# Output projection to second FFN layer on one core: split weights get one place, the last layer begins where the operands lay, in three passes instead of two

## The chip, the core and the metric

The kernel runs on one core of a Trainium2 chip. The core has five engines that work side by side, each through its own list of instructions in order: TensorE (PE in the profile; PEld is its weight load), VectorE (DVE), ScalarE (ACT), GpSimd (POOL) and SyncE (SP, which here only starts transfers). Transfers between the chip's memory (DRAM) and the on-chip memory (SBUF) run on 16 DMA engines. Matrix products land in PSUM, eight banks of 2 KB per partition. The metric is the device time of one execution in microseconds (us); lower is better.

## The reference, cut to what matters

One trunk layer over 128 prompt and 1024 sample tokens (1152 rows of 1024), then a final norm. Four mixing branches are gated and merged; the stretch that the change touches starts behind that:

```python
x = x + g1 * (merged @ w_o)
h = rmsnorm(x, norm2_g) * (1 + s2) + b2
a, b = split(h @ ffn_w1)                       # 2 x 2816 columns
x = x + g2 * ((silu(a) * b) @ ffn_w2)
y = rmsnorm(x, final_norm_g)
```

All of it is in float32. The kernel gets float32 accuracy out of a faster matmul type (fp32r) by splitting every operand into a high and a low part: a product is three matmuls, high x high, high x low and low x high. A split is a cast on ACT (the high part) and a subtraction on DVE (the low part).

## The kernel before, in words

A scheduler orders the instructions: the program text gives each a place, and pools of SBUF tiles with a fixed number of buffers decide who must wait for whom. A tile of a pool is handed on when its last reader is done. `M(...)` takes one of eight 4.6 KB tiles per partition that live from the gates to the first FFN layer; a queue's transfers start in the order in which they stand.

- **Gates** (line 1137 on). For each branch and each of eight column blocks j: gate product, branch product, tanh, sum into `merged[j]`. In the last branch each finished block is halved and split into `mhl[j]`, the stationary operand of the next stage.
- **Output projection, "wo"** (from line 1436). Three chunks c of 384 rows, two column halves hf, four pieces k2 of `w_o`. A piece is loaded (512 KB, line 1243), split (ACT 1244, DVE 1245) and used by 18 matmuls. Behind each half, DVE multiplies by g1 (1457), POOL adds to x (1458), ACT sums squares (1459). Behind each chunk x is stored to DRAM (`x_d`, line 1461, on SP), then normalised in place (1470 to 1473).
- **Transposes into quarters** (`norm_to_quarters`, line 1264 on): PE transposes ("ntr"), ACT writes `nv` (1279), DVE and POOL form differences `nu` (1283 to 1286), and seven operands are split into `xa` and `xb` (1289, 1290).
- **FFN1** (from line 1291): 22 pairs of column blocks, each as seven block products (a Strassen-like scheme that needs sums S1 to S4 of the weights, made on POOL, line 1318). `w_prepare` loads, sums and splits the weights of a product some products ahead (`LEAD`). Pair 0 is done for chunks 0 and 1 first, then for chunk 2; pairs 1 to 21 follow whole. `evac` empties the banks into `st`, `store` splits the result and writes it to DRAM (`hid_d`, line 1405).
- **FFN2** (from line 1494): two passes over 11 of the 22 row blocks of `w_ffn2` each; in a pass nine row tiles i, each 11 x 3 x 2 = 66 matmuls into two banks; DVE multiplies by g2 (1551), POOL (first pass) or DVE (second) adds to `acc`, which is x read back from DRAM. The last pass ends with the norm and the output.

Between wo and FFN1, and between FFN1 and FFN2, pools are closed and opened in the same SBUF: a new pool's tiles wait for what lay there. Lines of before that matter:

```python
w = load_o(A["w_o"][hf, k2], M("wraw", [P, 1024]) if c == hf == 0 and k2 < 2 else slot("wraw"))
dma(x1_d[3 * c + q], x1s[q])                       # on SP
dma(hid_d[q, :, :, self.j, :]..., f(hl[q])...)     # on SP
fctx.__exit__(None, None, None)                    # behind the last product of FFN1
xctx.__exit__(None, None, None)
zctx = tc.tile_pool(name="zp", bufs=1, reuse_waits="tile")   # FFN2's pool
```

Of the kernel before, what the change touches and what calls it, by code (L numbers as in the profile page):

```python
# [15 lines left out]
P = 128  # L16
# [20 lines left out]
LEAD = 4  # L37
PASSES = ((0, 11), (11, 22))
# [46 lines left out]
def kernel(ctx: ExitStack, tc: tile.TileContext, A: dict, O: dict):  # L85
# [13 lines left out]
    mctx = tc.tile_pool(name="mp", bufs=1)  # L99
# [1022 lines left out]
    merged, mhl = [], []  # L1122
# [12 lines left out]
    def gates(name, step):  # L1135
# [5 lines left out]
        for j in range(8):  # L1141
            w = load_w(A["w_gate"][b, j], 1280)
            if step == 1:
                merged.append(M("mg"))
                dma(merged[j], m_d[j])
# [16 lines left out]
            if step == 3:  # L1162
                hl = []
                for q in range(2):
# [3 lines left out]
                    else:  # L1168
                        hl.append(M("mhl", dt=F32R).rearrange("p (c n) -> p c n", c=NCH))
# [64 lines left out]
    rowctx = tc.tile_pool(name="rows", bufs=1, reuse_waits="tile")  # L1234
    rows = rowctx.__enter__()

    def slot(name, dt=F32, shape=(P, 1024)):
        return rows.tile(list(shape), dt, tag="w", name=nm(name), bufs=8)

    def load_o(src, raw):  # L1240
        hi, lo = slot("whi", F32R), slot("wlo", F32R)
        with ahead():
            dma(raw, src)
            S.copy(hi, raw)
            V.tensor_sub(lo, raw, f(hi))
        return hi, lo
# [4 lines left out]
    xa = (xp.tile([P, 4, NCH, 4, HALF], F32R, tag="hT_hi", name="xa_hi", bufs=1),  # L1251
          xp.tile([P, 4, NCH, 4, HALF], F32R, tag="hT_lo", name="xa_lo", bufs=1))
    xbv = [t.rearrange("p o c (k n) -> p o c k n", k=4) for t in xb]
    OPS = {"B11": (xa, 0), "B21": (xa, 1), "T1": (xa, 2), "T2": (xa, 3), "T3": (xbv, 0), "T4": (xbv, 1), "B22": (xbv, 2)}
# [11 lines left out]
    def norm_to_quarters(xn3, c):  # L1266

        cs = c * CH
        for kp in range(4):
            v = M("nv", [P, 2, 2, HALF])  # L1270
# [22 lines left out]
    def ring(name):  # L1293

        if "fp" in wide:
            return wide["fp"].tile([P, 2, 512], F32R, tag="wf", name=nm(name), bufs=11)
        return slot(name, F32R, (P, 2, 512))
# [25 lines left out]
    def w_prepare(j, i):  # L1323
# [10 lines left out]
        t = ring("wf")  # L1334
# [386 lines left out]
```

## Time and profile before

| | us |
|---|---|
| median of 3 runs (range) | 2164.93 (2162.74 to 2166.24) |
| the profiled execution, its span | 2166.64, 2164.9 |
| end of the gates' last matmul | 1208.5 |
| last wo matmul | 1340.4 |
| first matmul of pair 1 | 1385.5 |
| end of FFN1's last matmul | 1857.6 |
| first FFN2 matmul | 1874.9 |
| last FFN2 matmul | 2156.5 |

Times within a run are us from the span's start. In the trace names are shortened: f is a bank of FFN1 or FFN2, x the rows x1, w a split block of w_ffn2, mg a block of merged. A view of waits says which engine waited for whom and how long; a table of windows gives for chosen stretches the busy time of each engine, the granted TensorE clock (PEclk, 1.00 is 2.4 GHz and 0.50 is 1.2 GHz) and what the DMA engines moved.

### The profile page before, as it was taken

The numbers are of one execution on the slowest core, as the hardware profiler recorded it, in microseconds if no ns is written. First come the engines' busy times: TensorE is split into PE (matmuls) and PEld (weight loads), VectorE is DVE, ScalarE is ACT, GpSimd is POOL, SyncE is SP. The second block draws the span as 40 slices with busy tenths as digits, with TensorE's granted clock in tenths as the row PEclk, the third lists the DMA queues.
The fourth block names the chain that finished last, engine by engine and source line by source line (L and its number), as shares of the span: only waits on it lengthen the run. The fifth ranks groups of instructions, "written<-read, shape, count | busy, mean of one in ns | idle before, by whom it ended". The sixth has DMA issues, their size and how long they took to land. (4 is left out here: it accounts for less than half of the span.)

```text
span 2164.9 us, 31502 instructions
## 1 busy us (share of the span) xinstructions
PE 2065.0 (95%) x12400; PEld 1845.0 (85%) x12400; DVE 1191.1 (55%) x2105; ACT 738.6 (34%) x1320; POOL 374.5 (17%) x308
## 2 busy tenths in 40 slices
PE   6899999999999999999999799799999999699998
PEld 1558888998897899999999677799999999578886
DVE  4833499825443288998732368665665655230323
ACT  3734444445432523322222245433333333110200
POOL 1210020000001102232212135332232221011100
PEclk9999999999999999999999899899999999899999
DMA  7684552234142452332210344233233322652431
GB/s 282 206 276 147 194 185 96 67 103 142 59 153 85 131 180 83 99 127 69 99 49 25 127 157 164 85 109 104 93 105 93 113 95 62 258 212 106 174 121 66
DMA packets 172233, 276.21 MB, mean 128 GB/s; under 512 B 14546, under 2 KB 123699, under 8 KB 171956
## 3 DMA queue, kind: packets, MB, share of 16 engines
q1 hardware_dynamic: 172084, 274.19, 37.7%
q8 instruction: 97, 1.59, 0.3%
q14 instruction: 52, 0.43, 0.1%
HBM read 196.58 MB, written 77.56 MB: 127 GB/s over the span
## 5 line engine op out<-in xcount | busy, mean ns | idle before, releaser
L257 PE MATMUL gm<-hT_hi,whi 128*128 128x384 f32 x1224 | 420.1, 343 | 1.7 <-ACT sg L1155 1.7
L259 PE MATMUL gm<-hT_hi,wlo 128*128 128x384 f32 x1224 | 418.6, 342 | 0.7 <-DVE wlo L233 0.7
L258 PE MATMUL gm<-hT_lo,whi 128*128 128x384 f32 x1224 | 415.8, 340 | 0.0
L257 PEld LDWEIGHTS gm<-hT_hi,whi 128*128 128x128 f32 x1224 | 230.0, 188 | 12.5 <-issue 7.5
L259 PEld LDWEIGHTS gm<-hT_hi,wlo 128*128 128x128 f32 x1224 | 230.0, 188 | 9.2 <-issue 5.1
L258 PEld LDWEIGHTS gm<-hT_lo,whi 128*128 128x128 f32 x1224 | 230.0, 188 | 5.7 <-issue 3.8
L1367 PE MATMUL f<-xa_hi,wf 128*128 128x288 f32 (+2 forms) x704 | 209.6, 300 | 9.1 <-ACT wf L1336 9.1
L1368 PE MATMUL f<-xa_lo,wf 128*128 128x288 f32 (+2 forms) x704 | 211.1, 301 | 2.0 <-DVE xa_lo L1290 1.9
L1369 PE MATMUL f<-xa_hi,wf 128*128 128x288 f32 (+2 forms) x704 | 207.4, 299 | 0.2 <-DVE wf L1337 0.2
L257 PE MATMUL f<-w,hid 128*128 128x512 f32 x396 | 152.2, 396 | 22.2 <-DMA hid<-hid_d 17.3
L1160 POOL TENSOR_TENSOR mg<-mg,sg 128x384 f32<-128x384 f32 x72 | 96.5, 1340 | 363.8 <-DVE sg L1156 359.4
L1367 PE MATMUL f<-xb,wf 128*128 128x288 f32 (+2 forms) x528 | 157.3, 298 | 0.0
L1369 PE MATMUL f<-xb,wf 128*128 128x288 f32 (+2 forms) x528 | 157.1, 298 | 0.0
L1368 PE MATMUL f<-xb,wf 128*128 128x288 f32 (+2 forms) x528 | 157.1, 297 | 0.0
L259 PE MATMUL f<-w,hid 128*128 128x512 f32 x396 | 154.5, 393 | 1.0 <-DMA hid<-hid_d 1.0
L258 PE MATMUL f<-w,hid 128*128 128x512 f32 x396 | 155.2, 393 | 0.0
L1367 PEld LDWEIGHTS f<-xa_hi,wf 128*128 128x128 f32 x704 | 134.2, 191 | 9.4 <-ACT wf L1336 9.2
L1155 ACT ACTIVATE sg<-gm,vec 128x384 f32<-128x384 f32 x96 | 55.8, 581 | 241.1 <-PE gm L259 231.9
L1368 PEld LDWEIGHTS f<-xa_lo,wf 128*128 128x128 f32 x704 | 134.7, 191 | 2.7 <-DVE xa_lo L1290 2.7
L1369 PEld LDWEIGHTS f<-xa_hi,wf 128*128 128x128 f32 x704 | 133.8, 192 | 0.8 <-DVE wf L1337 0.8
L1156 DVE SCALAR_TENSOR_TENSOR sg<-sg,po 128x384 f32<-128x384 f32 x96 | 52.7, 549 | 122.8 <-PE po L259 117.2
L257 PEld LDWEIGHTS f<-w,hid 128*128 128x128 f32 x396 | 75.3, 191 | 39.7 <-issue 17.5
(350 smaller groups left out, 4169.0 us busy)
## 6 DMA issues: line engine op xcount, KB each, us to landing
hid_d<-hl SPq DMA_DIRECT2D x44, 576.0 KB
hid<-hid_d SPq DMA_DIRECT2D x36, 704.0 KB
adaw<-in_ada_w_dram SPq DMA_DIRECT2D x48, 512.0 KB
wraw<-in_w_ffn_dram SPq DMA_DIRECT2D x44, 512.0 KB
wraw<-in_w_gate_dram SPq DMA_DIRECT2D x32, 640.0 KB
wraw<-in_w_o_dram SPq DMA_DIRECT2D x24, 512.0 KB
w2r<-in_w_ffn_dram SPq DMA_DIRECT2D x22, 512.0 KB
wraw<-in_w_in_dram SPq DMA_DIRECT2D x19, 512.0 KB
```

Of the source, the lines that this page charges most:

```text
L257: mm(out, ah, bh, start=start, stop=False)
L258: mm(out, ah, bl, start=False, stop=False)
L259: mm(out, al, bh, start=False, stop=stop)
L1155: S.activation(sg, pg, AF.Tanh, bias=vc("gate_b", b * 8 + j), scale=0.5)
L1156: V.scalar_tensor_tensor(sg, sg, 1.0, po, op0=ALU.add, op1=ALU.mult)
L1160: G.tensor_add(merged[j][:, cs], merged[j][:, cs], sg)
L1367: mm(out, w[:, 0, ks], x[0], start=st, stop=False, skip_group_check=True)
L1368: mm(out, w[:, 0, ks], x[1], start=False, stop=False, skip_group_check=True)
L1369: mm(out, w[:, 1, ks], x[0], start=False, stop=sp_, skip_group_check=True)
```

## The change

One pool `fp`, opened behind the gates, serves from wo to the end: ten 4 KB slots ("wf"), three 2 KB halves ("ws") and two tiles "nv". It takes the place of the pools `rows` (wo) and `fp` (FFN1). The large tiles of FFN1 (raw weights, `st`, `hl`) now come from the eight M tiles; `LEAD` falls from 4 to 3. The first two pieces of w_o are loaded and split inside the last gates, the last two blocks of mhl lie in the unused quarter of xa, and w_prepare(0, 0..2) stands among the last wo pieces. The first three products of pair 1 are prepared right behind pair 0. Stores of hid go out on ACT's queue into three DRAM tensors, stores of x and the loads of acc on POOL's queue. In FFN2 the pool z opens in xa's place three products before FFN1 ends, hid and the first six blocks of w_ffn2 are loaded there, further blocks go to the slots and to xb's place, and there are three passes of 6, 8 and 8 blocks. In the last pass the squares are written to the half slot.

```diff
-LEAD = 4
-PASSES = ((0, 11), (11, 22))
+LEAD = 3
+PASSES = ((0, 6), (6, 14), (14, 22))
+            if step == 3 and j == 7:
+                first_o.extend(load_o(0, k2, M) for k2 in range(2))
...
-                        hl.append(M("mhl", dt=F32R).rearrange("p (c n) -> p c n", c=NCH))
+                        hl.append(xa[n // 2 % 2][:, 3, :, (n % 2) * CH:(n % 2 + 1) * CH])
...
-    rowctx = tc.tile_pool(name="rows", bufs=1, reuse_waits="tile")
+    fctx = tc.tile_pool(name="fp", bufs=1, side="right", reuse_waits="tile")
+    def slot(name, shape=(P, D), dt=F32):
+        return fp.tile(list(shape), dt, tag="wf", name=nm(name), bufs=10)
+    def half_slot(name):
+        return fp.tile([P, 512], F32, tag="ws", name=nm(name), bufs=3)
+    def quarters(name):
+        return fp.tile([P, 4 * HALF], F32, tag="nv", name=nm(name), bufs=2)
...
-            v = M("nv", [P, 2, 2, HALF])
+            v = quarters("nv").rearrange("p (i h n) -> p i h n", i=2, h=2)
-            u = M("nu", [P, 4, HALF])
+            u = [half_slot("nu")[:, :CH].rearrange("p (i n) -> p i n", i=2) for _ in range(2)]
...
+        ts_ = [M("wraw", [P, D]) for _ in range(2)]
...
+        t = half_slot("ws") if name < "S3" else quarters("ws")[:, :512]
...
-                dma(hid_d[q, :, :, self.j, :].rearrange("i p n -> p i n"),
+                nc.scalar.dma_start(hid_d[n][q, :, :, self.j - a, :].rearrange("i p n -> p i n"),
...
+                if c == NCH - 1 and hf == 1 and k2:
+                    w_prepare(0, k2 - 1)
+                w = first_o.pop(0) if first_o else load_o(hf, k2, slot)
...
-                t = rows.tile([P, 512], F32, tag="xt", name=nm("xt"), bufs=2)
+                t = half_slot("xt")
...
-            dma(x1_d[3 * c + q], x1s[q])
+            nc.gpsimd.dma_start(x1_d[3 * c + q], x1s[q])
...
+    for i in range(LEAD):
+        w_prepare(1, i)
...
+        if (j, i) == (NF - 1, 3):
+            xctx.__exit__(None, None, None)
+            open_z()
+            for i2 in range(6):
+                if i2 < 3:
+                    hid_load(0, i2)
+                w2_load(i2)
...
+                    acc.append(M("acc", [P, D]) if i2 < 8 else slot("acc"))
+                    nc.gpsimd.dma_start(acc[i2], x1_d[i2])
...
-                if n == 0:
+                if n < len(PASSES) - 1:
                     G.tensor_add(acc[i][:, hs], acc[i][:, hs], t)
```

How the instructions stand, in three places. First, SP's queue at the end of the gates, of before: behind the last two gate weights (`in_w_gate`) stand x, the g1 rows and then the pieces of w_o.

```order
L231 DMA wraw_11041<-in_w_gate_dram 128x1280 [waits DMAHW3_49,DMAHW7_49,DVE_49,PE_49]
L231 DMA wraw_11159<-in_w_gate_dram 128x1280 [waits DMAHW0_49,DMAHW4_49,DVE_49,PE_49]
L1442 DMA x_2056_11301<-in_x_all_dram 128x1024 [waits DMAHW1_49,Pool_49]
L1442 DMA x_2057_11302<-in_x_all_dram 128x1024 [waits DMAHW2_49,PE_49,Activation_49]
L1442 DMA x_2058_11303<-in_x_all_dram 128x1024
L1257 DMA g1r_11296<-mod_d 128x1024
L1257 DMA g1r_11297<-mod_d 128x1024 [waits DMAHW5_49,Activation_49]
L1243 DMA wraw_11313<-in_w_o_dram 128x1024 [waits DMAHW6_49,Activation_49]
```

The same place in the changed kernel:

```order
L1126 DMA wraw_11165<-in_w_o_dram 128x1024 [waits DMAHW5_49,DVE_49]
L231 DMA wraw_10809<-in_w_gate_dram 128x1280 [waits DMAHW6_49,PE_49]
L231 DMA wraw_10925<-in_w_gate_dram 128x1280 [waits DMAHW7_49,PE_49]
L1126 DMA wraw_11171<-in_w_o_dram 128x1024 [waits DMAHW0_49,DMAHW5_49,DVE_49,Activation_49]
L231 DMA wraw_11041<-in_w_gate_dram 128x1280 [waits DMAHW3_49,DMAHW1_49,PE_49]
L231 DMA wraw_11159<-in_w_gate_dram 128x1280 [waits DMAHW4_49,DMAHW2_49,PE_49]
L1268 DMA g1r_11304<-mod_d 128x1024 [waits DMAHW0_49,DVE_49,Activation_49]
L1268 DMA g1r_11305<-mod_d 128x1024 [waits DVE_49]
L1126 DMA wraw_11353<-in_w_o_dram 128x1024 [waits Pool_49]
L1452 DMA x_2070_11401<-in_x_all_dram 128x1024 [waits DMAHW6_49,DVE_49]
```

Two pieces of w_o moved ahead of the last gate weights, and the third ahead of x; the fourth stands behind four loads of x.

Second, POOL's list in the last half of chunk 2 of wo, of before: the sums S1 and S2 of pair 0 (ws, line 1318) stand behind the additions to x (line 1458) and the differences nu.

```order
L1458 TENSOR_TENSOR x_2174_11987<-x_2174_11987,xt_12101 128x512 [waits DMAHW0_49,DVE_49,PE_49]
L1285 TENSOR_TENSOR nu_11972<-nv_11961 128x192 [waits DVE_49,Activation_49]
L1286 TENSOR_TENSOR nu_11972<-nv_11961,nu_11972 128x192 [waits DVE_49]
L1318 TENSOR_TENSOR ws_12229<-wraw_12223 128x512 [waits DMAHW3_49,DMAHW4_49,DMAHW2_49,PE_49]
L1318 TENSOR_TENSOR ws_12229<-ws_12229,wraw_12222 128x512 [waits DMAHW2_49,Pool_49]
```

In the changed kernel (sums at line 1316, additions at 1457):

```order
L1316 TENSOR_TENSOR ws_12248<-wraw_12138,wraw_12139 128x512 [waits DMAHW1_49,DMAHW2_49,DVE_49,Pool_49]
L1296 TENSOR_TENSOR nu_12080<-nv_12068 128x192 [waits DVE_49]
L1297 TENSOR_TENSOR nu_12080<-nv_12068,nu_12079 128x192
L1457 TENSOR_TENSOR x_2194_12093<-x_2194_12093,xt_12099 128x512 [waits DMAHW7_49,DVE_49]
L1316 TENSOR_TENSOR ws_12169<-wraw_12139 128x512 [waits DVE_49]
L1457 TENSOR_TENSOR x_2195_12094<-x_2195_12094,xt_12103 128x512 [waits DMAHW0_49,DVE_49]
L1457 TENSOR_TENSOR x_2196_12095<-x_2196_12095,xt_12107 128x512 [waits DVE_49]
L1316 TENSOR_TENSOR ws_12171<-ws_12169,wraw_12138 128x512 [waits Activation_49]
```

The last row is S2 (pair 0's second product). It stands behind three additions, and it waits for ACT to free one of the three half slots; PE's second product of pair 0 now stands between the second and the third wo piece of that half.

Third, SP's queue at the end of FFN1, of before: behind the last stores of hid stand the first loads of FFN2.

```order
L1405 DMA hid_d<-hl_17366 128x9x128 [waits DMAHW3_49,Activation_49]
L1405 DMA hid_d<-hl_17367 128x9x128 [waits DMAHW4_49,DVE_49]
L1513 DMA w2r_17387<-in_w_ffn_dram 128x1024 [waits DMAHW5_49,PE_49]
L1513 DMA w2r_17392<-in_w_ffn_dram 128x1024 [waits DMAHW6_49]
L1257 DMA g2r_2758_17384<-mod_d 128x1024 [waits DMAHW7_49]
L1257 DMA g2r_2759_17385<-mod_d 128x1024 [waits DMAHW0_49]
L1535 DMA fng_17386<-in_final_g_dram 128x1024 [waits DMAHW1_49]
L1522 DMA hid_17445<-hid_d 128x1408 [waits DMAHW2_49,Pool_49]
```

And in the changed kernel; the row above the first hid load is the last raw weight of FFN1, and the PE instruction that the first hid load waits for is the last matmul that reads xa, 72 matmuls (three products) before the end of FFN1:

```order
L1311 DMA wraw_17027<-in_w_ffn_dram 128x1024 [waits DMAHW3_49,DVE_49,Pool_49]
L1520 DMA hid_17256<-hid_d 128x768 [waits DMAHW2_49,PE_49]
L1520 DMA hid_17256<-hid_d 128x768
L1126 DMA w2r_17259<-in_w_ffn_dram 128x1024 [waits DMAHW4_49]
L1520 DMA hid_17264<-hid_d 128x768 [waits DMAHW5_49]
L1520 DMA hid_17264<-hid_d 128x768 [waits DMAHW6_49]
L1126 DMA w2r_17267<-in_w_ffn_dram 128x1024 [waits DMAHW7_49]
L1520 DMA hid_17272<-hid_d 128x768 [waits DMAHW0_49]
```

The stores are gone from this queue, and hid and w_ffn2 alternate; the rows g2r and fng come later.

## Rows read from the trace of the kernel before

**Rows 1.** The head of the profile's page.

```profile
span 2164.9 us, 31502 instructions
```

**Rows 2.** The view of waits of PE, in three stretches (1190 to 1345, 1345 to 1395, 1840 to 2165): who waited for whom, us in total, how often, the longest.

```profile
PE wo L257 <- ACT whi L1244: 14.0, 1, 14.0
...
PE wo L257 <- ACT nv L1279: 7.3, 2, 4.0
...
PE f L1367 <- ACT wf L1336: 9.1, 1, 9.1
...
PE f L257 <- DMA hid<-hid_d: 17.3, 1, 17.3
...
PE f L257 <- ACT w L1515: 4.9, 2, 3.4
```

**Rows 3.** Windows: length, busy us (instructions) of PE, PEld, DVE, ACT, POOL; then the granted clock, the busy share of the DMA engines, GB/s.

```profile
1222.50:1226.00 3.50, 3.46 (x8) 2.65 (x9) 3.45 (x3) 2.10 (x2) 0.00 (x0) 0.50 0.50 204
...
1322.20:1325.10 2.90, 2.90 (x7) 2.32 (x8) 2.15 (x3) 2.78 (x6) 2.31 (x3) 0.50 0.94 363
...
1385.50:1390.00 4.50, 4.50 (x18) 4.28 (x19) 1.18 (x2) 1.18 (x3) 3.76 (x4) 0.50 0.26 105
...
1400.00:1830.00 430.00, 430.00 (x3232) 430.00 (x3231) 261.27 (x312) 143.80 (x233) 110.54 (x77) 1.00 0.31 98
...
1858.00:1874.00 16.00, 0.00 (x0) 0.00 (x0) 5.06 (x6) 2.76 (x3) 0.00 (x0) 0.60 0.86 289
...
1875.00:1878.00 3.00, 3.00 (x7) 2.30 (x8) 0.00 (x0) 0.00 (x0) 0.00 (x0) 0.50 1.02 421
...
1899.00:1905.00 6.00, 5.61 (x13) 4.45 (x14) 2.43 (x2) 1.38 (x2) 0.00 (x0) 0.50 0.48 165
```

**Rows 4.** The end of the gates in the timelines of POOL, SP and ACT: start, us, instruction, count, and in brackets the idle time before it and what ended that.

```profile
1209.34 0.99 POOL L1160 TENSOR_TENSOR mg<-mg,sg 128x384 f32<-128x384 f32 x1 [4.19 <-DVE sg L1156]
...
1210.36 1.28 SPq L1442 DMA_DIRECT2D x<-in_x_all_dram  x3
...
1211.69 1.01 SPq L1257 DMA_DIRECT2D g1r<-mod_d  x2
...
1212.80 16.23 SPq L1243 DMA_DIRECT2D wraw<-in_w_o_dram  x5
...
1221.44 1.04 ACT L1244 CAST whi<-wraw 128x1024 fp32r<-128x1024 f32 x1 [9.91 <-DMA wraw<-in_w_o_dram]
```

**Rows 5.** PE's timeline: two wo matmuls 18 apart, and two of pair 0's 384 column matmuls 22 apart.

```profile
1331.85 0.40 PE L258 MATMUL wo<-wlo,xb 128*128 128x512 f32 x1
...
1336.05 0.40 PE L259 MATMUL wo<-whi,xb 128*128 128x512 f32 x1
...
1340.56 0.34 PE L1368 MATMUL f<-xa_lo,wf 128*128 128x384 f32 x1
...
1344.41 0.33 PE L1369 MATMUL f<-xa_hi,wf 128*128 128x384 f32 x1
```

**Rows 6.** Around the second boundary between chunks of wo, and POOL's work for x and for pair 0: timelines of PE, ACT and POOL.

```profile
1322.20 0.79 PE L257 MATMUL wo<-whi,xb 128*128 128x512 f32 x1 [3.27 <-ACT nv L1279]
...
1321.48 1.23 ACT L1279 ACTIVATE nv<-ntr,modv,amul 128x384 f32<-128x384 f32 x2
...
1323.54 0.51 ACT L1289 CAST xa_hi<-nv 128x384 fp32r<-128x384 f32 x1
...
1323.95 0.35 ACT L1289 CAST xb<-nv 128x192 fp32r<-128x192 f32 x1
...
1299.04 4.78 POOL L1458 TENSOR_TENSOR x<-x,xt 128x512 f32<-128x512 f32 x3 [9.40 <-DVE xt L1457]
...
1337.24 1.29 POOL L1318 TENSOR_TENSOR ws<-wraw 128x512 f32<-128x512 f32 x1 [4.58 <-DMA wraw<-in_w_ffn_dram]
```

**Rows 7.** From the end of chunk 0's last half to its third normalised row tile (PE, DVE), the same tile of chunk 2, a DVE instruction beside a POOL addition, and the store of x on SP.

```profile
1299.21 0.40 PE L259 MATMUL wo<-whi,mhl 128*128 128x512 f32 x1
...
1307.69 0.75 DVE L1473 TENSOR_SCALAR x<-x,wst 128x1024 f32<-128x1024 f32 x1 [0.66 <-POOL wst L280]
...
1352.55 0.75 DVE L1473 TENSOR_SCALAR x<-x,wst 128x1024 f32<-128x1024 f32 x1 [0.20 <-POOL wst L280]
...
1326.69 1.45 DVE L1290 TENSOR_TENSOR xb<-nv,xb 128x192 fp32r<-128x192 f32 x1
...
1341.32 7.40 SPq L1461 DMA_DIRECT2D x_d<-x  x3
```

**Rows 8.** Between pair 0 and pair 1: timelines of DVE, SP and ACT.

```profile
1377.11 1.58 DVE L1403 TENSOR_TENSOR hl<-st,hl 128x576 fp32r<-128x576 f32 x2
...
1381.11 1.30 SPq L1308 DMA_DIRECT2D wraw<-in_w_ffn_dram  x3
...
1384.81 0.62 ACT L1336 CAST wf<-wraw 128x512 fp32r<-128x512 f32 x1 [6.91 <-DMA wraw<-in_w_ffn_dram]
```

**Rows 9.** Between FFN1 and FFN2: SP's and PE's timelines, and the DMA view of 1870 to 1880 (packets, MB, share of 16 engines; KB of one transfer).

```profile
1859.95 1.15 SPq L1405 DMA_DIRECT2D hid_d<-hl  x2
...
1864.87 0.91 SPq L1522 DMA_DIRECT2D hid<-hid_d  x2
...
1874.93 0.76 PE L257 MATMUL f<-w,hid 128*128 128x512 f32 x1 [17.30 <-DMA hid<-hid_d]
...
q1 hardware_dynamic: 869, 3.91, 97.0%
```

More of the change, by code (lines that the diff above doesn't have):

```diff
@@ L1119, in hyena, with load_hl, load_o @@
         yield 2.0
-    merged, mhl = [], []
+    merged, mhl, first_o, xa = [], [], [], []
+    def load_hl(raw, hi, lo, src):
+        dma(raw, src)
+        S.copy(hi, raw)
+        V.tensor_sub(lo, raw, f(hi))
+        return hi, lo
+    def load_o(hf, k2, place):
+        with ahead(1000):
+            return load_hl(place("wraw", [P, D]), place("whi", [P, D], F32R), place("wlo", [P, D], F32R), A["w_o"][hf, k2])
     wcol = {"hy": 0, "mla": 1, "ret": 2, "conf": 3}
@@ L1233 @@
     wctx.__exit__(None, None, None)
-    rowctx = tc.tile_pool(name="rows", bufs=1, reuse_waits="tile")
[L1235 to L1254, printed above, removed]
+    fctx = tc.tile_pool(name="fp", bufs=1, side="right", reuse_waits="tile")
+    fp = fctx.__enter__()
+    def slot(name, shape=(P, D), dt=F32):
[4 more added lines that the diff above has]
+        return fp.tile([P, 4 * HALF], F32, tag="nv", name=nm(name), bufs=2)
+    xav, xbv = ([t.rearrange("p o c (k n) -> p o c k n", k=4) for t in ts_] for ts_ in (xa, xb))
+    OPS = {"B11": (xav, 0), "B21": (xav, 1), "T1": (xav, 2), "T2": (xav, 3), "T3": (xbv, 0), "T4": (xbv, 1), "B22": (xbv, 2)}
     def bcast_row(dst, cnd, part):
@@ L1290, in norm_to_quarters @@
                 V.tensor_sub(lo, src, f(hi))
[L1293 to L1297, printed above, removed]
+            yield
     PRODUCTS = (("A11", "B11"), ("S2", "T2"), ("A12", "B21"), ("S1", "T1"), ("S3", "T3"), ("S4", "B22"), ("A22", "T4"))
@@ L1394, in store @@
         def store(self):
-            shape = [P, NCH, 2, HALF]
-            if "fp" in wide:
-                hl = [wide["fp"].tile(shape, F32R, tag="hl", name=nm("hl"), bufs=2) for _ in range(2)]
-            else:
-                hl = [M("hl", shape, F32R) for _ in range(2)]
+            hl = [M("hl", [P, NCH, 2, HALF], F32R) for _ in range(2)]
             for h in range(2):
@@ L1436, in first_pair @@
             pair0.evac(i, view, sel)
+    late = iter(())
     for c in range(NCH):
-        x1s = [rows.tile([P, D], F32, tag="x1", name=nm("x1"), bufs=3) for _ in range(3)]
         sts = [small("wst", [P, 4], bufs=4) for _ in range(3)]
-        for q in range(3):
-            dma(x1s[q], A["x_all"][3 * c + q])
         for hf in range(2):
@@ L1484, with open_z, zt, w2_place @@
     four = psum["left", "ctx"].__enter__()
-    fctx = tc.tile_pool(name="fp", bufs=1, reuse_waits="tile")
-    wide["fp"] = fctx.__enter__()
+    z, w2, hid = {}, {}, {}
+    def open_z():
+        z["ctx"] = tc.tile_pool(name="zp", bufs=1, reuse_waits="tile")
+        z["pool"] = z["ctx"].__enter__()
+    def zt(tag, shape, bufs, dt=F32):
+        return z["pool"].tile(list(shape), dt, tag=tag, name=nm(tag), bufs=bufs)
+    def w2_place(j):
+        if j < 4 or 14 <= j < 18:
+            t = zt("w2", [P, 2, D], 4, F32R)
+            return t[:, 0], t[:, 1]
+        if 6 <= j < 12 or j == 21:
+            i, n = divmod(j - 6, 3) if j < 12 else (0, 0)
+            if n == 0:
+                z[i] = wide["right"].tile([P, 3, 2, D], F32R, tag=f"xb{i}", name=nm("w2"), bufs=1)
+            return z[i][:, n, 0], z[i][:, n, 1]
+        return tuple(slot("w2", dt=F32R) for _ in range(2))
+    def w2_load(j):
+        if j in w2:
+            return
+        w2[j] = load_hl(zt("w2r", [P, D], 4), *w2_place(j), A["w_ffn2"][j])
+    def hid_load(n, i):
+        if n == len(PASSES) or (n, i) in hid:
+            return
+        a, b = PASSES[n]
+        t = zt("hid", [P, 2, 8, P], 3, F32R)
+        for q in range(2):
+            dma(f(t[:, q, :b - a]), hid_d[n][q, i])
+        hid[n, i] = t[:, 0], t[:, 1]
     order = [(j, i) for j in range(1, NF) for i in range(7)]
-    for n in range(LEAD):
-        w_prepare(*order[n])
     pairs = {}
```

116 lines of the change are left out of this document (48 added, 68 removed).

## Prediction

> **What bounds the kernel now.** I read the page first, then PE's waits, then windows with the granted clock, then the timelines of the engines on both sides of each wait. The span is 2164.9 us [rows 1]; the profiled execution took 2166.64 us, so 1.7 us lie outside it, and it is 1.7 us above the median of the runs shown. PE is the bound: in the main loop of FFN1 it is busy 430 of 430 us at clock 1.00, with DVE at 61% and ACT at 33% [rows 3]. The change leaves the number of matmuls as it is. It can gain only where PE waits, and behind 1200 us that is at five places: 14.0 us from the gates to wo, 7.3 us at the two chunk boundaries, 9.1 us from pair 0 to pair 1, 17.3 us from FFN1 to FFN2 and 4.9 us in the first row tiles of FFN2 [rows 2]. Each such pause also leaves PE at 0.50 for a while: 3.5, 2.9, 4.5, 3.0 and 6.0 us in the windows behind them [rows 3], and half of such a window is lost work (1.75, 1.45, 2.25, 1.5, 3.0). That is what can be won: 52.6 us of waits and about 11.4 us of clock (the boundary's 1.45 counted twice).
>
> **Gates to wo.** In before the last merged block is done at 1210.3, only then x, g1 and w_o are asked for, and the first piece is cast at 1221.44 [rows 4]. Now two pieces are split before the gates end (one ACT cast and one DVE subtraction each, in gates in which PE alone is full; I cost them at nothing, and at most 2.3 us each if they delay a gate). PE goes from the gates into 36 wo matmuls of 0.233 us (18 in 4.20 us) [rows 5], 8.4 us. The third piece still waits for the last merged block (1210.3) but is then first in SP's queue: it is there some 3 us later and split 2.3 us after that, about 1216, before PE wants it at 1216.9. The fourth stands behind four loads of x; at the 391 GB/s of a full stretch (3.91 MB in 10 us) [rows 9] it is the sixth transfer of 0.52 MB behind 1210.3, 8.0 us plus some 2 to start and land; its high part is cast (1.04) near 1221.5 and its low part ready near 1222.7, about 1 us late; the fifth, behind two more loads of x, is about 0.5 us late. So -14.0 - 1.75 + 1.5 = **-14.2 us** (bounds -16.5 and -9, the latter if the third and fourth piece come as late as the first did behind the same x).
>
> **Chunk boundaries.** PE waits there for ACT to empty transpose banks: four nv (1.23 us for two), then the high casts of 0.51 and 0.35 us, before the next nv [rows 6]. The order still has the transposes in two bunches, with four and then twelve or more before a wo matmul that needs their banks. Same list on ACT, same wait: **0** (-3 to +3: the nv and nu tiles are now rings of two and three).
>
> **Last half of wo.** Here is the new wait that I expect. Pair 0's products stand among the wo pieces, and its second product needs S2, which POOL makes behind S3, two nu, three additions to x and S1. From the boundary's first transposes on, POOL can begin that row of work when ACT has done eight nv (4.9), nine casts (4.4), one weight cast and DVE one subtraction: 10.7 us. Then S3, S1 and S2 at 1.29, the nu at what I put at 0.8 each, and additions of 1.6 (4.78 for three) [rows 6]: 10.3 us; S2 is cast at 21.6. PE arrives sooner: 41 wo matmuls (9.6 us), 12 products of 384 columns at 0.175 (3.85 us for 22) [rows 5] (2.1), transposes some 1.8, the boundary's wait 3.3 and about 1 us of smaller ones, 17.8. So 4.0 us of waiting and, as behind the 3.3 us boundary, 1.5 us of clock: **+5.5** (0 to +8).
>
> **Pair 0 to pair 1.** From the last wo matmul to pair 1 before took 45.1 us (1340.4 to 1385.5), with the clock 47.35. 40 of the 84 wide products of pair 0 now lie ahead, 7.0 us, which leaves 40.35 to compare. After: from the end of a half to the third normalised x tile chunk 0 took 9.2 us (1299.2 to 1308.4), plus POOL issuing three stores between its additions and its powers, an operation that before does not have. Its price lies between nothing and 2.5 us each (SP's three in 7.40) [rows 7]; I take 2 us for all three, near POOL's shorter instructions. Then 22 us to the end of pair 0 (before: 1353.3 to 1376.4, 23.1, with PE held by other products in between). PE has only 7.7 us of other work (44 products) in the first 11.2, and stands idle for most of the rest: cover that the old order had is gone, but the chain through ACT is the same. Pair 1's raw weights were asked for only at 1381.1, behind the hid stores [rows 8]; now they come during the chain. But ACT now issues the store of the low half, which waits for DVE until 1378.7, and only then casts pair 1's first weights (0.62): 3.3 us of wait instead of 9.1, with 1.5 of clock. 11.2 + 22 + 3.3 + 1.5 = 38.0 against 40.35: **-2.4** (-10 to +6).
>
> **FFN1's loop.** LEAD 3 still leaves 9.6 us (three products of 24 matmuls at 0.133) for a cast of 0.62 us [rows 8] and a subtraction of about that length, the raw tiles are asked for a whole pair ahead, and a store on ACT's queue delays ACT, which is idle two thirds of the time [rows 3]. **0** per pair; the bound above is a rival below.
>
> **FFN1 to FFN2.** Before, hid and w_ffn2 could be asked for only when FFN1's pool had closed; first hid loads at 1864.9, PE at 1874.9, DMA 86% busy in between [rows 3, 9]. Now the loads start when the last reader of xa is done, 9.6 us before FFN1's end. At 391 GB/s hid(0), w0, hid(1) and w1 (2.6 MB) need 6.7 us plus some 2 to land, so PE can go on; hid(2), w2 to w5 (2.9 MB) follow in 7.4 us, and the order lets i = 0, 1, 2 share each block, so a new block is wanted only every 4 us at the start. I charge 1.0 us for the bank that the last evacuation of pair 21 still holds and a late block. -17.3 - 4.9 - 1.5 - 3.0 + 1.0 = **-25.7** (-28 to -16: the hid stores of the last two pairs share the DMA engines). The later blocks go to slots and to xb's place with a pass of 50 us or more to spare; the nine more evacuations lie on DVE and POOL: 0 to +3.
>
> **Sum.** -14.2 + 0 + 5.5 - 2.4 + 0 - 25.7 = -36.8 us on 2166.6, that is 2129.8, and 1.7 less against the median: **2128 us**, 1.7% faster.
>
> **A rule against it.** In the trace DVE and POOL hinder each other: a DVE subtraction of 128x192 took 1.45 us beside a POOL addition [rows 7]. The Trainium skill's page "SBUF — State Buffer", section "SBUF: two separate sides", goes further: while DVE runs an instruction that holds the shared ports, GpSimd cannot write the descriptors of a transfer issued from its queue. No run here has such a transfer yet. By that rule the x stores would be late and the normalised rows with them, which gives the third rival's 2136 where the sum has 2128.
>
> **Rivals.**
> 1. FFN1's loop gets a gap in every pair: raw weights come too late for S1, S2, because eight M tiles hold raws, st and hl of two pairs, or ACT stands at a store. For it: 7 of 8 tiles are in use per pair. Against it: every wait in the order points a pair back. A sum, a cast and a subtraction (1.29 [rows 6], 0.62 [rows 8] and, I take, 0.7) exposed each time give 2.6 x 21 = 55 us: 2183, slower. It decides from 1.75 us per pair (36.8 / 21).
> 2. FFN2's loads come late after all, as w did in before (4.9 us) plus a wait for hid and the clock: +10, 2138.
> 3. POOL's stores, held up by DVE, make the third x tile 8 us later (the 7.40 us of before's stores, once more): 2136. At the earlier chunks 12 us of wo cover it.
> 4. The early loads do not start early (a wait for something that ends with FFN1): of 25.7 nothing stays, 2154.
>
> **Chances.** Forecast 0.62 (its own range 2116 to 2141), rivals 0.08, 0.10, 0.12 and 0.04, and 0.04 for a better end (no S2 wait, the shorter chain: 2114). With the bounds of the terms the range is 2110 to 2152. About 0.2% (4 us) is what a measurement can tell from no change. Faster 0.90, same 0.02, slower 0.08.
>
> **What would show it.** In the new profile: no wait between gates and wo above 1.5 us; a wait of PE for ACT's wf cast in the last half of wo, led by POOL's ws; a wait for x before the last transposes; 3 us before pair 1; FFN1 at 100%; no wait above 2 us at FFN2's start and clock 1.00 there. A busy share under 100% in FFN1 or a wait for hid above 5 us makes the forecast wrong.

## The result, and the profile after

The changed kernel takes 2148.56 us, the median of 4 runs (2141.68 to 2150.53), against 2164.90, now the median of 4 runs (the table of the kernel before has 3 of them, 2164.93); the ratio is 0.992 with a 95% interval of 0.9896 to 0.9943. It is faster by 0.8%, which is 16.3 us where the sum gave 36.8. The profiled execution took 2148.07 us.

The runs differ mostly ahead of the change: the gates end at 1208.5 us before, at 1207.2 after, and anywhere between 1205.1 and 1212.9 in the experiments. So I compare stretches, counted from the gates' end, by the ends of PE's matmuls. The 7.0 us that 40 products of pair 0 take, which now stand among the wo pieces, are counted with pair 0 in both columns.

| stretch, us | before | after | difference | forecast |
|---|---|---|---|---|
| gates' end to the end of wo's chunk 0 | 49.3 | 40.4 | -9.0 | -14.2 |
| to the first half of chunk 2 | 60.4 | 60.1 | -0.3 | 0 |
| to the last wo matmul | 22.3 | 32.3 | +10.1 | +5.5 |
| to the end of pair 1 | 69.7 | 69.7 | 0.0 | -2.4 |
| to the end of FFN1 | 447.3 | 447.0 | -0.3 | 0 |
| to the last FFN2 matmul | 298.9 | 280.7 | -18.2 | -25.7 |

These give -17.7; with the gates' 1.3 us they are the 19.0 us by which the span fell. All that was won ahead of FFN1 was lost again there; the gain is FFN2's.

The page's head and the views of PE's waits in the three stretches of [rows 2]; columns as there:

```profile
span 2145.9 us, 31575 instructions
...
PE wo L257 <- ACT nv L1290: 6.1, 2, 3.5
PE f L1364 <- ACT wf L1334: 4.0, 1, 4.0
PE wo L257 <- ACT whi L1127: 3.2, 1, 3.2
PE wo L258 <- DVE wlo L1128: 2.8, 4, 1.3
...
PE f L1364 <- ACT wf L1334: 4.7, 2, 3.5
...
PE f L257 <- DVE st L1388: 2.1, 1, 2.1
PE f L257 <- DMA hid<-hid_d: 2.1, 1, 2.1
```

The waits of 14.0, 9.1 and 17.3 us are gone. In their place stand 3.2 us for a piece of w_o, 4.0 and 3.5 us for split weights of FFN1, and two of 2.1 us at FFN2's start. The windows of the changed kernel, columns as in [rows 3]:

```profile
1224.00:1227.40 3.40, 3.10 (x8) 2.47 (x8) 0.30 (x1) 1.05 (x1) 0.00 (x0) 0.51 0.73 293
...
1329.80:1336.80 7.00, 6.54 (x18) 5.37 (x19) 3.15 (x4) 3.29 (x6) 0.87 (x1) 0.52 0.00 0
...
1384.50:1387.90 3.40, 3.40 (x16) 3.40 (x16) 0.00 (x0) 0.00 (x0) 0.00 (x0) 0.52 1.09 370
1400.00:1830.00 430.00, 430.00 (x3234) 430.00 (x3233) 212.18 (x307) 129.69 (x225) 96.72 (x76) 1.00 0.33 100
1858.00:1874.00 16.00, 13.97 (x61) 11.53 (x62) 9.57 (x11) 7.75 (x9) 1.59 (x3) 1.00 1.04 395
```

FFN1's loop is full as before. FFN2 begins at clock 1.00, with the DMA engines full. Behind the wait for pair 0's second product PE stands at about half clock for 7.0 us, where I had allowed 1.5 us of loss.

### The profile page after: what moved, and what is told of

Same layout as the page of the kernel before. It is cut to its first block, busy times and chain, and to the rows that moved or that the text cites. A ratio compares the mean times of both kernels' runs of the same rounds, so it can differ in the third digit from the quotient of the medians.

```text
span 2145.9 us, 31575 instructions
## 1 busy us (share of the span) xinstructions
PE 2070.2 (96%) x12400; PEld 1844.4 (86%) x12400; DVE 1158.8 (54%) x2123; ACT 727.2 (34%) x1320; POOL 406.5 (19%) x344
## 3 DMA queue, kind: packets, MB, share of 16 engines
q1 hardware_dynamic: 120692, 238.80, 32.9%
## 4 chain that ended last, share of the span: by engine, by line
PE 86%; DVE 5%; DMA 4%; ACT 2%; issue 1%; SPq 1%; POOL 1%; ACTq 0%; DVEq 0%; POOLq 0%
PE gm L257 9%; PE gm L259 9%; PE gm L258 9%; PE f L1365 8%; PE f L1366 8%; PE f L1364 7%; PE f L259 4%; PE f L258 4%; PE f L257 4%; PE po L682 2%; PE ptr L672 2%; PE po L258 1%; PE po L259 1%; PE po L257 1%; PE wo L258 1%
## 5 line engine op out<-in xcount | busy, mean ns | idle before, releaser
L1570 DVE TENSOR_TENSOR fin<-f,g2r 128x512 f32<-128x512 f32 x54 | 37.1, 690 | 156.0 <-PE f L259 152.9
```

The costliest lines, as they stand in the source:

```text
L1570: V.tensor_mul(t, pts[hf], g2rows[i == 8][:, hs])
```

## Experiments: what the second layer lost

In FFN2 the waits are short, and still 7.5 us are missing. The spacing of the matmuls tells why: 512 columns took 0.2267 us in before on every block of w_ffn2, but 0.2333 in the changed kernel on blocks 4 to 13 and 18 to 21, which lie in the slots and in xb's place, while blocks 0 to 3 and 14 to 17, in z, kept 0.2267. Four runs shift pools by some bytes and do nothing else; a fifth lines all of them up.

**The right-hand pools 32 bytes lower.**

```diff
+    lead = tc.tile_pool(name="lead", bufs=1, side="right")
+    lead.__enter__().tile([P, 8], F32, name="lead")
     mctx = tc.tile_pool(name="mp", bufs=1, side="right")
...
     mctx.__exit__(None, None, None)
+    lead.__exit__(None, None, None)
```

> All right-hand pools lie 32 bytes lower, so that every operand begins at a multiple of 64 bytes; nothing else changes. In the changed kernel a 512-column matmul of the second layer takes 0.2333 us where its weight block lies in a right-hand pool (blocks 4 to 13 and 18 to 21) and 0.2267 us where block and activations both lie in the left-hand one. Theory P (what counts is whether stationary and moving operand begin at the same place within 64 bytes): all blocks 0.2267; 14 blocks x 9 row tiles x 6 = 756 matmuls x 0.0066 = -5.0 us in the second layer, -0.7 us in the output projection (108 matmuls on xa), up to -2 us in the first layer: 2140 to 2143 us. Rival S (what counts is the half of the memory, or the distance): the blocks keep their two times, 2148 us.

2147.57 us (ratio to before 0.9919, 0.9898 to 0.994), and both times per matmul stayed. A place within 64 bytes is not it.

**The pool z 480, 96 and 224 bytes higher** (the diff for 480; 24 and 56 columns for the others).

```diff
         z["pool"] = z["ctx"].__enter__()
+        z["pool"].tile([P, 120], F32, name="lead")
```

> The second layer's own pool (activations, raw weights, blocks 0 to 3 and 14 to 17) begins 480 bytes higher, so that its tiles stand at the same place within 512 bytes as the right-hand pools; nothing else changes. The shift by 32 bytes left the two times per matmul as they were, which rules out the place within 64 bytes, but not within a larger unit: at a shift of 32 the right-hand pools still stood 64 bytes off within 128, and 448 within 512. Theory P2 (what counts is the same place within 128, 256 or 512 bytes): all 22 blocks 0.2267 us, -5.0 us in the second layer. Rival S (the region that an operand lies in, or how regions pair): blocks 4 to 13 and 18 to 21 stay at 0.2333, 2148 us or by the spread of single runs 2142 to 2150.

> The same pool begins 96 bytes higher: the same place within 128 bytes as the right-hand pools, another within 256 and 512. Theory P2 with a unit of 128: all blocks 0.2267 us; with a unit of 256 or 512: two times as before the shift. Rival S: two times as before, like the shift by 480.

> The second layer's own pool begins 224 bytes higher: the same place within 256 bytes as the right-hand pools, another within 512. A shift by 480 gave 0.2267 us per 512 columns on all 22 blocks, a shift by 96 left blocks 4 to 13 and 18 to 21 at 0.2333. Unit of 256: all blocks 0.2267, -5.0 us in the second layer. Unit of 512: the two times stay.

By 480: 2140.34 us, all 22 blocks at 0.2267. By 96: 2144.31 us, the two times as in the changed kernel. By 224: 2143.84 us, all blocks at 0.2267. DVE's multiplications by g2 mark the row tiles of the second pass, each 48 matmuls; first of the changed kernel:

```profile
1970.03 1.39 DVE L1570 TENSOR_TENSOR fin<-f,g2r 128x512 f32<-128x512 f32 x2 [9.81 <-PE f L259]
1981.23 1.39 DVE L1570 TENSOR_TENSOR fin<-f,g2r 128x512 f32<-128x512 f32 x2 [9.81 <-PE f L259]
```

The same with z shifted by 480 bytes:

```profile
1965.90 1.37 DVE L1571 TENSOR_TENSOR fin<-f,g2r 128x512 f32<-128x512 f32 x2 [9.51 <-PE f L259]
1976.78 1.37 DVE L1571 TENSOR_TENSOR fin<-f,g2r 128x512 f32<-128x512 f32 x2 [9.51 <-PE f L259]
```

And by 224:

```profile
1969.43 1.37 DVE L1571 TENSOR_TENSOR fin<-f,g2r 128x512 f32<-128x512 f32 x2 [9.51 <-PE f L259]
1980.31 1.37 DVE L1571 TENSOR_TENSOR fin<-f,g2r 128x512 f32<-128x512 f32 x2 [9.51 <-PE f L259]
```

11.20 us are 48 times 0.2333, 10.88 are 48 times 0.2267. The right-hand pools begin 480 bytes behind a multiple of 512, z begins at a multiple. The quick time comes when the stationary operand (hid) and the moving one (w_ffn2) stand at the same place within 256 bytes, as at shifts of 480 and 224; at 96 they differ by 128 within 256, in the changed kernel by 224, in the first run by 192. FFN1's end to FFN2's end fell from 280.7 us (279.9 to 283.9 in runs that leave FFN2 alone) to 276.0 and 276.3. In before, hid and all blocks lay in one pool, each at a multiple of 512.

**All pools in line.** The pool of xb gets 480 bytes at its end, which also moves the slots below it.

```diff
     xb = [wide["right"].tile([P, 3, NCH, 4 * HALF], F32R, tag=f"xb{q}", name=f"xb{q}", bufs=1) for q in range(2)]
+    wide["right"].tile([P, 120], F32, name="tail")
```

> The right-hand pool with the upper part of the operands' place gets 480 bytes at its end, so that it and the slots below it begin at a multiple of 512 bytes, as the left-hand pools do; nothing else changes. Theory P2 (both operands at the same place within 512 or 256 bytes: 0.2267 us per 512 columns, otherwise 0.2333): second layer 0.2267 on all 22 blocks, as when its own pool was moved to the others' place, -5.0 us; output projection 0.2267 on xa too, -0.7 us; first layer, if its 288-column matmuls (0.1325 to 0.1346 in the changed kernel) follow the same rule, down to 0.1325, -2 us; together 2140 to 2143 us. Rival: only the second layer follows, 2143 to 2144 us.

2144.10 us (2143.39 to 2145.43; ratio to before 0.9899, 0.9883 to 0.9916). FFN2 is at 0.2267 throughout, wo on xa fell from 0.233 to 0.228, FFN1's 447.04 us to 446.04: half of what I had allowed there. The time stays just above the 2140 to 2143 us of the forecast: FFN2's stretch shows only 3.3 us less, because its second wait was 4.5 us in this run.

**That second wait.** In the changed kernel it is for the activations of the fourth row tile. SP's timeline of the changed kernel there:

```profile
1852.40 15.58 SPq L1126 DMA_DIRECT2D w2r<-in_w_ffn_dram  x7
...
1876.14 0.33 SPq L1126 DMA_DIRECT2D w2r<-in_w_ffn_dram  x1
1880.43 0.80 SPq L1520 DMA_DIRECT2D hid<-hid_d  x2
```

Four of the weight loads ahead of it (blocks 6 to 9) are for the second pass, and they wait for buffers, so the load of hid starts only 23.7 us behind FFN1's end. Two runs: the loads of hid on GpSimd's queue, and the weight loads paced.

```diff
-            dma(f(t[:, q, :b - a]), hid_d[n][q, i])
+            nc.gpsimd.dma_start(f(t[:, q, :b - a]), hid_d[n][q, i])
```

> The second layer's loads of activations go through GpSimd's queue, not SyncE's, where the fourth row tile's load was issued at 1880.4 us behind weight loads that waited for raw buffers. Theory F (that queueing is the second wait of 2.1 us, and up to 4.5 us in other runs): the wait at 1884 us goes, -2 us, first layer's end to second layer's end 278.5 us instead of 280.7. Rival (the transfers themselves are late, since the DMA engines are full there): a wait of 2 us or more stays at the same row tile.

```diff
             h = hid.pop((n, i))
+            if n + 1 < len(PASSES) and PASSES[n + 1][0] + i < PASSES[n + 1][1]:
+                with tc.issue_after(last["hid"].ins):
+                    w2_load(PASSES[n + 1][0] + i)
```

> The weight blocks of the second and the third pass are loaded one per row tile, each behind that tile's load of activations; before, SyncE's queue held the weight loads of blocks 6 to 9 ahead of the fourth row tile's activations. Theory F (they held the load, issued at 1880.4 us, though its buffer came free at 1868): no wait above 0.5 us at the fourth row tile, first layer's end to second layer's end 278.3 us instead of 280.7, and no new wait at the passes' beginnings. Rival (the transfers, with the DMA engines full): 2 us stay, as with the loads on GpSimd's queue.

On GpSimd's queue: 2153.66 us, the first wait 5.6 us, the second 2.7; FFN2's stretch 286.8. The wait stayed, as the rival had it, but this run does not show the rival's reason: on GpSimd's queue the load stood behind a load of acc that waited for a store of hid, and started even later, 28.8 us behind FFN1's end. POOL's timeline of this run:

```profile
1884.12 0.53 POOL L1565 DMA_DIRECT2D acc<-x_d  x1 [16.61 <-DMA hid_d<-hl]
1884.73 1.08 POOL L1520 DMA_DIRECT2D hid<-hid_d  x2
```

Paced: 2151.4 us in a run whose gates ended 5.7 us later than in the changed kernel. The load of hid started 16.8 us behind FFN1's end, FFN2 took 277.2 us, and PE's waits behind 1850 us were

```profile
PE f L257 <- DVE st L1388: 2.1, 1, 2.1
```

So it was the order of the loads: of the two 2.1 us only the last bank's is left. Pacing also takes other transfers away at that time; whether full DMA engines had a share in the wait, no run here separates.

## Experiments: what was lost ahead of the first layer

Kernels whose edits lie elsewhere show how far these stretches vary by themselves: chunk 0 38.3 to 40.4 us, the last half (pair 0's products included) 37.8 to 39.7, from there to pair 1's end 62.8 to 63.8.

**x behind the pieces.** SP's timeline of the changed kernel behind the gates: six loads of x around the fourth piece.

```profile
1210.20 0.33 SPq L1126 DMA_DIRECT2D wraw<-in_w_o_dram  x1
1210.63 3.44 SPq L1452 DMA_DIRECT2D x<-in_x_all_dram  x4
1214.13 0.42 SPq L1126 DMA_DIRECT2D wraw<-in_w_o_dram  x1
1215.18 1.24 SPq L1452 DMA_DIRECT2D x<-in_x_all_dram  x2
```

PE waited there for the fourth piece and for the low part of the fifth (the expectation below calls it the sixth). The fifth piece's high part was there at 1226.9, but its subtraction stood on DVE behind two multiplications by g1, which waited for PE. Timelines of DVE and PE:

```profile
1228.10 1.39 DVE L1456 TENSOR_TENSOR xt<-wo,g1r 128x512 f32<-128x512 f32 x2 [3.80 <-PE wo L259]
1229.41 1.98 DVE L1128 TENSOR_TENSOR wlo<-wraw,whi 128x1024 fp32r<-128x1024 f32 x1
...
1231.45 0.50 PE L258 MATMUL wo<-wlo,xb 128*128 128x512 f32 x1 [1.29 <-DVE wlo L1128]
```

```diff
-                for q in range(3):
-                    dma(x1s[q], A["x_all"][3 * c + q])
+                with tc.issue_after(last["wo"].ins):
+                    for q in range(3):
+                        dma(x1s[q], A["x_all"][3 * c + q])
...
-        dma(raw, src)
+        last["wo"] = dma(raw, src)
```

> The loads of x of a chunk are held behind the chunk's fourth piece of w_o on the DMA queue; before, three of chunk 0 and three of chunk 1 stood around the fourth piece's load. Theory A (the fourth and the sixth piece waited 3.2 and 1.3 us, and 1.7 us went to half clock, because 3 MB of x went ahead of them): chunk 0's first half loses nothing, chunk 0 ends 5 to 6 us earlier, 2142 to 2144 us. Rival (the pieces are late because they are first issued at 1210.2 us, when the gates' buffers come free): the fourth piece still waits 2 us or more, 2146 to 2148 us.

2144.64 us. PE's waits from 1190 to 1240 us, all of them:

```profile
PE wo L258 <- DVE wlo L1128: 0.2, 1, 0.2
```

Chunk 0 took 33.4 us instead of 40.4. The fourth piece's load was issued 3.4 us behind the gates' end instead of 6.9, and the fifth piece's subtraction now stands ahead of the multiplications on DVE, so both waits went. But at pair 1's end hardly anything of it was left (200.5 us behind the gates' end, where kernels without this edit have 199.8 to 203.6): the chains below gave it back. The gates of this run ended 2.1 us earlier, which is most of what its time shows.

**Pair 0's weights behind the last piece.**

```diff
-                if c == NCH - 1 and hf == 1 and k2:
-                    w_prepare(0, k2 - 1)
...
-            for i in range(3, 7):
+            for i in range(7):
```

> The first three weight products of pair 0 are prepared behind the output projection's last piece again, as before the change; the rest of the change stays. Theory C (the last half lost time because pair 0's second product stood among the pieces and waited 4.0 us for S2, and 3.4 us to half clock behind it): the last piece ends at 1333 to 1336 us instead of 1350.7, and the first pair ends 5 to 7 us earlier, 2141 to 2143 us. Rival (the time only moves: pair 0's products wait for their weights behind the last piece): the first pair ends within 2 us of 1379.9, 2147 to 2150 us.

2143.89 us. The last piece ended at 1333.4, and from the end of chunk 2's first half to pair 1's end it took 92.4 us, as before the change (92.0); in the changed kernel 102.1. The early preparation alone cost those 9.7 us. What takes its place in this run's waits (1300 to 1420 us):

```profile
PE ntr L1286 <- DVE x L1471: 6.8, 2, 5.0
PE f L1364 <- ACT wf L1334: 4.7, 2, 3.5
```

**S1 and S2 in a slot of their own.** POOL's and ACT's timelines of the changed kernel: S1 (at 1324.35) stands behind an addition and then waits for a half slot that DVE frees; S2 (at 1328.05) comes behind two more additions.

```profile
1317.07 1.49 POOL L1316 TENSOR_TENSOR ws<-wraw,wraw 128x512 f32<-128x512 f32 x1 [2.21 <-DVE xb L1301]
...
1321.19 2.20 POOL L1457 TENSOR_TENSOR x<-x,xt 128x512 f32<-128x512 f32 x1 [0.90 <-DVE xt L1456]
1324.35 1.29 POOL L1316 TENSOR_TENSOR ws<-wraw 128x512 f32<-128x512 f32 x1 [0.96 <-DVE xb L1301]
1325.60 2.48 POOL L1457 TENSOR_TENSOR x<-x,xt 128x512 f32<-128x512 f32 x2
1328.05 1.25 POOL L1316 TENSOR_TENSOR ws<-ws,wraw 128x512 f32<-128x512 f32 x1
...
1329.34 0.62 ACT L1334 CAST wf<-ws 128x512 fp32r<-128x512 f32 x1 [0.50 <-POOL ws L1316]
```

```diff
-        t = half_slot("ws") if name < "S3" else quarters("ws")[:, :512]
+        if j == 0 and name < "S3":
+            if name == "S1":
+                raws[j]["sums"] = slot("ws")
+            t = raws[j]["sums"][:, 512 * (name == "S2"):][:, :512]
+        else:
+            t = half_slot("ws") if name < "S3" else quarters("ws")[:, :512]
```

> S1 and S2 of pair 0 get a slot of their own instead of two of the three half slots that they share with the norm's differences and the projection's products. Theory B (S1 came at 1324.4 us because its half slot came free then, and S2 behind it): S1 starts at 1318 to 1319 us, S2's cast by 1323, the wait of 4.0 us at 1326 goes and most of the half clock behind it: last piece 4 to 7 us earlier, 2142 to 2145 us. Rival (POOL's own queue, the adds into x that wait for VectorE, holds S2): the wait stays above 3 us, 2147 to 2149 us.

2141.33 us, the last half 34.9 instead of 39.4. The same work in this run:

```profile
1317.24 1.40 POOL L1321 TENSOR_TENSOR ws<-wraw 128x512 f32<-128x512 f32 x1
1318.60 2.26 POOL L1462 TENSOR_TENSOR x<-x,xt 128x512 f32<-128x512 f32 x1
1320.82 1.59 POOL L1321 TENSOR_TENSOR ws<-ws,wraw 128x512 f32<-128x512 f32 x1
...
1322.44 0.62 ACT L1339 CAST wf<-ws 128x512 fp32r<-128x512 f32 x1 [0.83 <-POOL ws L1321]
```

The sums no longer wait for a buffer, and PE does not wait for the cast there at all. But POOL's list stands otherwise too: S1 ahead of all three additions and S2 behind one, where one stood ahead of S1 and three ahead of S2. How much of the gain is the buffer's and how much the order's, this run does not separate. Two of the 40 products of pair 0 (0.35 us) also moved behind the last piece.

**Pair 1's weights before pair 0's store.** ACT's timeline of the changed kernel: the first cast of pair 1 stands behind the two transfers, the second behind a copy that waits for PE.

```profile
1381.42 1.22 ACTq L1399 DMA_DIRECT2D hid_d<-hl  x2
1382.68 0.62 ACT L1334 CAST wf<-wraw 128x512 fp32r<-128x512 f32 x1 [1.29 <-DVE hl L1396]
1388.83 0.64 ACT L1374 COPY st<-f 128x576 f32<-128x576 f32 x1 [5.53 <-PE f L1366]
1389.37 0.62 ACT L1334 CAST wf<-ws 128x512 fp32r<-128x512 f32 x1
```

```diff
-    pair0.store()
     for i in range(LEAD):
         w_prepare(1, i)
+    pair0.store()
```

> Pair 1's first three weight products stand ahead of pair 0's store in the program, no longer behind it. Theory D (pair 1 waited 3.5 us, because its first cast stood behind the store's casts and its two transfers on ScalarE's queue until 1382.7 us, though its raw weights had landed by 1370.6): pair 1 starts within 1 us of pair 0's end and takes 23 to 25 us instead of 26.2, together -3 to -6 us. Rival (the splits now stand ahead of the rescales of the last rows of x on VectorE and hold them up): the first pair ends 1 us or more later, and the gain is lost.

2139.29 us. From the last wo matmul to pair 1's end 57.5 us instead of 62.8; pair 1 began 0.45 us behind pair 0.

**x stored from SyncE again.** Timelines of POOL and DVE in the changed kernel at the end of chunk 1: POOL issues the stores behind all three additions and the rescales in place wait for them.

```profile
1291.78 4.77 POOL L1457 TENSOR_TENSOR x<-x,xt 128x512 f32<-128x512 f32 x3 [3.63 <-DVE xt L1456]
1296.49 1.13 POOL L1460 DMA_DIRECT2D x_d<-x  x2
...
1299.61 0.75 DVE L1473 TENSOR_SCALAR x<-x,wst 128x1024 f32<-128x1024 f32 x1 [1.09 <-DMA x_d<-x]
...
1302.73 0.75 DVE L1473 TENSOR_SCALAR x<-x,wst 128x1024 f32<-128x1024 f32 x1 [0.46 <-DMA x_d<-x]
```

```diff
-            nc.gpsimd.dma_start(x1_d[3 * c + q], x1s[q])
+            dma(x1_d[3 * c + q], x1s[q])
```

> Only the stores of x go back to SyncE's queue. With the five edits together this took the first pair's end from 166.5 to 156.9 us behind the first matmul of the output projection. Theory X (GpSimd's queue costs the changed kernel too): the first pair's end comes 3 us or more earlier than 172.8 us behind that matmul. Rival (in the changed kernel other waits, above all pair 0's second product, stand in front of the chain): within 2 us of 172.8.

2143.99 us; the first pair ended 165.9 us behind that matmul, 6.9 earlier. The timelines of POOL, SP and DVE of this run at the same place:

```profile
1287.53 4.85 POOL L1457 TENSOR_TENSOR x<-x,xt 128x512 f32<-128x512 f32 x3 [4.25 <-DVE xt L1456]
...
1288.84 0.33 SPq L1460 DMA_DIRECT2D x_d<-x  x1
1291.16 1.57 SPq L1460 DMA_DIRECT2D x_d<-x  x2
...
1292.92 0.76 DVE L1473 TENSOR_SCALAR x<-x,wst 128x1024 f32<-128x1024 f32 x1 [0.33 <-POOL wst L280]
```

SP issues each store as its addition ends. The third rescale ends 9.2 us behind chunk 1's last matmul instead of 13.6, and the last half takes 35.0 us instead of 39.4.

## A version that beats both

**Five edits together**, then **with x on SyncE**: pools in line, w_ffn2 paced, pair 0's weights behind the last piece, x behind the fourth piece, pair 1's weights before the store; the second kernel adds the last edit above.

> Five edits together: places by 480 bytes, w2 paced, pair 0's weights behind the last piece, x behind the fourth piece, pair 1's weights before pair 0's store. If each kept what it gave alone against the changed kernel (-5.7, -2.1, -10.3 at the first pair's end, -2.6, -6.7): up to -27 us, 2121 us. But the chain behind the last piece (x, its norm, chunk 2's products) sets the first pair's end where pair 0's weights no longer hold it, and what x behind the pieces gave must show there in full: 2121 to 2127 us. Rival (edits in one stretch overlap: pair 1's weights ahead of the store then stand in front of the chain on VectorE): 2128 to 2133 us.

> The five edits, and the stores of x back on SyncE's queue. In the run with pair 0's weights behind the last piece, two rescales of chunk 2 waited for the store of x, which GpSimd had issued at 1336.6 and 1338.9 us between its other work; the third rescale ended 11.7 us behind the last piece. Theory X (GpSimd's queue costs the chain): the third rescale ends within 9.5 us of the last piece, first pair 1.5 to 2.5 us earlier than with the five edits alone. Rival (the store's transfer, not its queue, is what the rescale waits for): within 0.7 us of the five edits alone.

The five give 2123.54 us (2120.09 to 2125.28; ratio to before 0.9801, 0.9787 to 0.9816), as expected for a stretch that the chain through x then bounds. With x on SyncE it is **2114.86 us** (2113.83 to 2117.8; ratio 0.9766, 0.9751 to 0.978), 50.7 us under the kernel before in the same runs and 33.7 under the changed one's median above. The third rescale of chunk 2 ends 8.2 us behind the last piece (11.4 with the five alone), but the first pair gained 9.6 us, not 1.5 to 2.5: the chains of the earlier chunks became shorter too. From the gates' end to pair 1's end it needs 180.0 us (before 201.8, changed 202.5), FFN1 446.0, FFN2 272.1. PE's longest waits that are left there, from 1200 to 1420 us:

```profile
PE wo L258 <- DVE wlo L1128: 7.2, 4, 4.8
PE ntr L1287 <- DVE x L1473: 4.6, 2, 4.1
```

## Why the prediction was wrong

- **What bounds the kernel, and FFN1's loop at 0**: right, 430 of 430 us again. Rivals 1 and 4 fell: no gap per pair, and the first hid was there when PE came. Of the signs named beforehand two failed, the bounds of 1.5 us between gates and wo (3.2) and of 2 us at FFN2's start (2.1, twice); the others came. The bounds of the terms add up to 2107 to 2160 us; the stated range is narrower.
- **Gates to wo, -14.2, measured -9.0.** The steps that failed are "about 1 us late" for the fourth piece and "about 0.5 us" for the fifth. The fourth piece's high part was cast by 1223.0, 1.5 us behind the 1221.5 of the forecast; and PE stood there at 1219.9, 1.2 us before the 1221.1 that the forecast's terms give, because the gates ended 1.3 us earlier and 18 matmuls took 4.1 us, not 4.20 [rows 5] (xb and its weights stood at different places before, at the same one after). So it waited 3.2 us, for the fifth piece 1.3, and 0.5 us more for two low parts: 4.9 where 1.5 were charged. The clock behind it (3.4 us at 0.51, so 1.7 lost) was charged at nothing. Together that is 5.1 of the 5.2 us. For the fourth piece x ahead of it was the cause, as the run with x behind the pieces shows: chunk 0 7 us shorter, all of the -14.2 and more. The fifth piece was not late by its transfer, but by its place in DVE's list, which that run moved as well.
- **Chunk boundaries, 0**: -0.3. The sum was right, a part was not: the x chain inside became 4 to 5 us longer (chunk 1, whose rows [rows 7] puts down to chunk 0: 8.8 us from the last matmul to the third rescale's end before, 13.6 after) and was passed on to the last half.
- **Last half of wo, +5.5, measured +10.1.** The wait for S2 was named, and its 4.0 us came out, but in part by luck. The forecast's own terms give 21.6 - 17.8 = 3.8; counted from the transposes at 1305.2 us, S2 was cast after 24.8 us and PE stood there after 20.8, both 3 us later than forecast. What failed is the loss to the clock behind it (7.0 us at 0.52, so 3.4 instead of 1.5), and three waits of 0.4, 1.1 and 0.25 us around it that I had not counted; they add up to +9.2, and 0.9 us are not assigned. I put S2's lateness down to POOL's work alone; the late stores of x were in it too, and a shared half slot with the order that came with it, as the two runs show that took 4.4 and 4.5 us off this stretch. These gains overlap: each moves the same S2 ahead of the same wait.
- **Pair 0 to pair 1, -2.4, measured 0.0.** Chain (32.9 us to the end of pair 0, forecast 33.2), wait (3.45, forecast 3.3) and clock (1.7, forecast 1.5) came out; missing was that pair 1's second product would wait as well (1.25 us). The other 1.1 us of the 2.4 are not assigned.
- **FFN1 to FFN2, -25.7, measured -18.2.** The early loads did what the sum says. Three terms were missed or mis-sized: the matmuls themselves, taken as unchanged, became 5.0 us longer; the last bank took 2.1 us where 1.0 was charged; and the fourth row tile waited 2.1 us (and 0.4 once more) behind weights that rival 2 had in mind. Together that is 8.6 us, 1.1 more than the 7.5 that are missing.
- **Third rival and the rule beside it.** Stores late by 4 to 5 us did happen, and "at the earlier chunks 12 us of wo cover it" was wrong. But the trace gives another mechanism than the rule in the Trainium skill ("SBUF — State Buffer", section "SBUF: two separate sides"): the stores were issued late, because they stood in GpSimd's queue behind the additions (issue at 1296.49, the end of the third addition), and 3.1 us later the first rescale could start. Whether descriptors were held up besides, no run here separates.

The four shortfalls (5.2, 4.6, 2.4, 7.5) are 19.7 us; less 1.3 for the gates and 0.6 for boundaries and loop, plus the 0.4 by which the time outside the span grew, they are the 18.2 us between the forecast's 36.8 and the 18.6 of the profiled runs.

## What to carry to other kernels

Give both operands of a matmul the same place within 256 bytes when a pool is moved: a pad of some hundred bytes was worth 5 us here. A transfer that is put on a compute engine's queue starts when its turn comes there; if something waits for the transfer (an in-place operation for the store of its tile, the next cast), count all that stands ahead. Work that fills a gap in front of the last critical pieces must have its inputs sooner than PE arrives, down to the buffers of its helpers, or it makes a longer gap than it fills.

## What the runs showed of the hardware

A 512-column fp32r matmul issued every 0.2267 us when stationary and moving operand began at the same place within 256 bytes, and every 0.2333 us at the differences tried (128, 192 and 224); other differences, and why it is so, are open. The Trainium skill ("SBUF — State Buffer", section "SBUF: two separate sides") says that on the engine side PE does not wait for another engine; these 3% are no other engine's doing, since they follow the block within one stretch, and that section does not let one expect them. For the 288-column matmuls of FFN1 the effect was 1.0 us in 447 with all pools in line, and 0.7 us the other way (447.73) with the right-hand pools 32 bytes lower.
